# POOL's arithmetic moved to VectorE throughout a two-layer backbone, and a new order in the second half of the first layer's MLP

## The chip, the core and the metric

The kernel runs on one core of a Trainium2 chip. Its engines work side by side: TensorE (PE; its weight loads are listed apart as PEld), VectorE (DVE), ScalarE (ACT), GpSimd (POOL) and SyncE (SP). Each takes its own instructions strictly in order; waits between engines go over semaphores. A transfer is started by an instruction on one of the queues of SP, ACT or POOL and then runs by itself. The metric is the device time of one run in microseconds (us), as a median of several runs. Beside them there is one profiled execution, from which all durations of single instructions come.

## The reference

A backbone of two layers works on 1024 latent tokens (x) and 256 context tokens (ctx) of width 1024, all in fp32. Each layer computes, with adaLN shifts, scales and gates `m` from a conditioning vector (`mc` for the context, from a learned vector):

```python
h  = modulate(rmsnorm(x, g[0]), m[0], m[1]);  hc = modulate(rmsnorm(ctx, g[0]), mc[0], mc[1])
y, yc = mixer(h, hc, ...)       # layer 0: gated linear attention (GLA) | grouped-query attention with
                                # normed, rotated heads; layer 1: long convolution (hyena) | diff. attention
x = x + m[2] * rmsnorm(y, g[1])
x = x + m[5] * rmsnorm(sq_relu_mlp(modulate(rmsnorm(x, g[2]), m[3], m[4]), w_mlp_in[i], w_mlp_out[i]), g[3])
# layer 0 alone: the same two sums for ctx, with mc
def sq_relu_mlp(h, w1, w2): return jnp.square(jax.nn.relu(h @ w1)) @ w2    # 1024 -> 4096 -> 1024
```

Only x is returned.

## The kernel before

PE multiplies in a format (fp32r) that keeps fewer bits than fp32. So each fp32 operand is split in two: ACT rounds it to the high part, and another engine subtracts that from the source, which leaves the low part (`split`, L92 to L95). A product is then the sum of three matmuls, high by high, low by high, high by low (L103 to L105, L1515 to L1517). With a third argument `split` puts the subtraction on POOL, otherwise on DVE.

The stages follow one another along the span, with soft borders:

- 0 to 300 us: layer 0's norm, its input projection, the normed heads and their rotation. `head_norm` (L485 to L488) multiplies by the root mean square on DVE and by the gain on POOL; `rope` (L603 to L619) makes one product on DVE (L611), two half products on POOL (L616) and the sum of the two on POOL (L618). In these tiles `stg` is a block out of the projection, `rp_o` and `rp_u` are the rotated parts, `q_st` is the split result. In the same stage the adaLN weights (`w_ada`) are summed up on DVE, row block by row block (L259, L261; `ada_rest`), with the low part of the sum (`ada_hl`, L227) on POOL. This `ada` work goes on in the background of later stages.
- 300 to 600 us: grouped-query attention. 600 to 1000 us: the spectra of hyena's filters (`hy_m` blocks come by DMAs on POOL's queue), the GLA (`gl_ee`, L927, `gl_aT`, L960, `gl_sg`, L1004 and L1008, all on POOL) and the output projection.
- 1000 to 1464 us: the residual sum (`post_norm`, L1061, on POOL for every second tile), the norm, and the first half of layer 0's MLP (`up_...`), in a scheme of seven products over half blocks in place of eight. `s1` to `s4` are sums of weight blocks on DVE (L1223), whose space POOL's splits of the weights (`w_lo<-up_w`) must have left.
- 1476 to 1895 us: the second half, `mlp_down` (L1414). It takes the seven products in the order p1, p2, p3, p5, p6, p7, p4, each over 16 blocks k, which makes 112 steps. A step loads a block of the hidden values (`dn_h`), one or two blocks of weights (`dn_b`), for four of the products a block of the context's hidden values (`dn_c`), takes differences of weight blocks where the product needs one (L1477), splits both and multiplies for four tiles of 128 rows. `load(i)` runs `bufs[0]` steps ahead, `prep(i)` two steps ahead. The tuple `bufs` (5, 6, 4, 6) counts the buffers of raw hidden blocks, raw weight blocks, context blocks and split pairs. The first two steps' loads go on ACT's queue, the rest on SP's. At a product's last block `put` adds its four banks of PSUM into the sums in SBUF (`accx`, `accy`; L1496). PSUM has five banks with the tag `dp` for the x tiles and two with `cx` for the context, which takes part in p1, p2, p3 and p5 only. During p7 and p4 the generator `ends` runs once in two blocks: for the two context tiles (`accz`) and then the first four x tiles it does the norm, the gate (L1060) and the residual sum (L1061). `dn_t` is the weight block that p5 loads and p6 and p4 use again.
- 1895 to 2100 us: layer 1's projection, with `cb_lo` (the low part of a column block of weights, by `w_block`) and `qk_lo` on POOL. 2100 to 2400: differential attention; 2400 to 2700: the convolution (its `hm` blocks come by POOL's queue, the out-projection's weights are split into `wo_lo` on POOL); 2700 to 3058: out-projection and first half of the MLP; 3058 to 3385: its second half.

The order in which instructions stand on each engine isn't that of the code. It is worked out when the kernel is built, from the instructions' dependences and estimated durations, so an operation that goes to another engine moves others as well. A tile's space comes free when its last reader is done, and a transfer into it waits for that.

Of the kernel before, what the change touches and what calls it, by code (L numbers as in the profile page):

```python
# [91 lines left out]
def split(g, hi, lo, src, pool=False):  # L92

    g.nc.scalar.activation(hi, src, ACTF.Copy)  # L94
    (g.nc.gpsimd if pool else g.nc.vector).tensor_tensor(lo, src, f(hi), op=ALU.subtract)  # L95
# [369 lines left out]
def in_proj0(g, ps, ftp, vgp):  # L465
# [12 lines left out]
    with ExitStack() as st:  # L478
# [6 lines left out]
        def head_norm(src, nh, gain):  # L485
            r = head_rstd(g, pq[0], src, nh, 64, f"rp_u{nh}")
            nc.vector.tensor_tensor(src, src, r.unsqueeze(2).to_broadcast([128, nh, 64]), op=ALU.mult)
            nc.gpsimd.tensor_tensor(src, src, gain.unsqueeze(1).to_broadcast([128, nh, 64]), op=ALU.mult)  # L488
# [117 lines left out]
def rope(g, pool, src, nh, t1, t2):  # L606
# [8 lines left out]
    for k in range(2):  # L615
        nc.gpsimd.tensor_tensor(uv[:, :, :, k], sv[:, :, :, 1 - k],  # L616
                                tv[:, :, k].unsqueeze(1).to_broadcast([128, nh, 32]), op=ALU.mult)
    nc.gpsimd.tensor_tensor(o, o, u, op=ALU.add)  # L618
# [207 lines left out]
def gla(g, st, y_put):  # L826
# [81 lines left out]
    def weights(t, b, p, la):  # L908
# [18 lines left out]
        nc.gpsimd.tensor_tensor(gate(ee), gate(ee), kb, op=ALU.mult)  # L927
# [23 lines left out]
    def inner(t, b, ee, kinT):  # L951
# [8 lines left out]
        nc.gpsimd.tensor_tensor(aT, ab[b][:, :, 0, :], ab[b][:, :, 1, :], op=ALU.add)  # L960
# [89 lines left out]
def post_norm(g, y, x_t, gate, tmp, junk, pool=True):  # L1050
# [10 lines left out]
    (nc.gpsimd if pool else nc.vector).tensor_tensor(x_t, x_t, tmp, op=ALU.add)  # L1061
# [1529 lines left out]
```

## Time and profile before

| | |
|---|---|
| median of 3 runs | 3390.24 us (3385.76 to 3394.58) |
| profiled execution | 3387.06 us |
| its span in the trace | 3385.3 us |
| mean granted clock of PE | 0.967 |
| busy: ACT | 1538.6 us (45%) |
| busy: DVE | 2489.5 us (74%), 4507 instructions |
| transfers | 566.69 MB, 167 GB/s over the span |

A row of the profile names the line of the code, the engine, the operation, output and inputs by the program's names with their shapes, and how often it occurs; behind the bar stand the busy time, the mean duration of one in ns, and the idle time of the engine just before, with the engine or transfer that ended it. In a timeline a row begins with start and duration in us, and brackets hold the idle time before. "issue" in a chain of waits is time in which an engine waited for nothing that the profile shows.

### The profile page before, as it was taken

The page shows a single profiled execution, that of the slowest core. Times are in us where ns is not written, and L with a number is a line of the kernel's source. Part 1 is how long each engine was busy: PE and PEld are TensorE (multiplying, and loading weights), DVE is VectorE, ACT ScalarE, POOL GpSimd, SP SyncE. Part 2 cuts the span into 40 slices and gives each one's busy share as a digit, 9 for nine tenths or more (in the row PEclk, how much of TensorE's full clock was granted, in tenths as well). Part 3 has the DMA queues.
Part 4 walks back from the last instruction along what each step waited for, and adds up shares of the span by engine and source line. Part 5 has one row for each costly group of instructions (what it writes and reads, how often), then busy time and mean ns, then how long its engine had stood idle before and what let it go on. Part 6 is the DMA issues. An engine that isn't in the chain of part 4 may idle for free.

```text
span 3385.3 us, 41884 instructions
## 1 busy us (share of the span) xinstructions
PE 3134.7 (93%) x13896; PEld 2405.3 (71%) x13896; DVE 2489.5 (74%) x4507; ACT 1538.6 (45%) x3150; POOL 528.0 (16%) x392
## 2 busy tenths in 40 slices
PE   8879999889987999989998899999968989999998
PEld 4766777667766788868876777766635667887886
DVE  6787767677658776766688666677778489877777
ACT  4444766554655222223345543576621352224453
POOL 0153000123222122201111112100020122210000
PEclk9999999999998999999999999999989999999999
DMA  6544111667753343378777455432344635438964
GB/s 227 154 129 147 55 40 47 178 193 228 244 199 114 132 146 131 134 255 297 240 245 241 135 167 168 116 97 74 122 142 135 226 113 168 146 137 303 314 194 161
DMA packets 344581, 566.69 MB, mean 167 GB/s; under 512 B 43329, under 2 KB 138561, under 8 KB 344236
## 3 DMA queue, kind: packets, MB, share of 16 engines
q1 hardware_dynamic: 296244, 491.19, 44.4%
q10 hardware_dynamic: 40952, 47.67, 4.1%
q0 software_dynamic: 7168, 25.17, 2.5%
q8 instruction: 109, 1.79, 0.2%
q14 instruction: 108, 0.88, 0.1%
HBM read 410.36 MB, written 153.55 MB: 167 GB/s over the span
## 4 chain that ended last, share of the span: by engine, by line
PE 63%; DVE 14%; issue 10%; DMA 7%; ACT 3%; POOL 3%; SPq 0%; ACTq 0%; POOLq 0%; DVEq 0%
PE up_ps L105 5%; PE up_ps L104 5%; PE up_ps L103 5%; PE dn_ps L1516 5%; PE dn_ps L1515 5%; PE dn_ps L1517 5%; PE s_ps L644 2%; PE up_ps L1234 1%; PE s_ps L738 1%; PE o_ps L2224 1%; DMA up_w<-in_w_mlp_in 1%; PE st_ps L758 1%; PE st_ps L759 1%; DVE ada_acc L261 1%; PE o_ps L771 1%
## 5 line engine op out<-in xcount | busy, mean ns | idle before, releaser
L1515 PE MATMUL dn_ps<-dn_w_hi,dn_h_hi 128*128 128x512 f32 x896 | 351.3, 394 | 28.2 <-DVE accy L1496 14.3
L1516 PE MATMUL dn_ps<-dn_w_lo,dn_h_hi 128*128 128x512 f32 x896 | 352.9, 394 | 5.3 <-DVE dn_w_lo L95 5.3
L1517 PE MATMUL dn_ps<-dn_w_hi,dn_h_lo 128*128 128x512 f32 x896 | 351.5, 392 | 0.0
L94 ACT ACTIVATE dn_h_hi<-dn_h 128x512 fp32r<-128x512 f32 x224 | 140.8, 629 | 279.4 <-PE dn_ps L1516 192.1
L95 POOL TENSOR_TENSOR w_lo<-up_w,w_hi 128x512 fp32r<-128x512 f32 x106 | 144.4, 1372 | 582.8 <-ACT w_hi L94 548.1
L95 DVE TENSOR_TENSOR dn_h_lo<-dn_h,dn_h_hi 128x512 fp32r<-128x512 f32 x224 | 161.9, 723 | 83.7 <-ACT dn_h_hi L94 83.3
L1515 PEld LDWEIGHTS dn_ps<-dn_w_hi,dn_h_hi 128*128 128x128 f32 x896 | 169.8, 190 | 67.7 <-DVE accy L1496 16.1
L1516 PEld LDWEIGHTS dn_ps<-dn_w_lo,dn_h_hi 128*128 128x128 f32 x896 | 170.1, 190 | 43.6 <-DVE dn_w_lo L95 8.5
L1517 PEld LDWEIGHTS dn_ps<-dn_w_hi,dn_h_lo 128*128 128x128 f32 x896 | 170.1, 190 | 35.4
L261 DVE SCALAR_TENSOR_TENSOR ada_acc<-w_ada,sc,ada_acc 128x512 f32<-128x512 f32 x224 | 169.0, 791 | 19.7 <-DMA w_ada<-in_w_ada 19.0
L94 ACT ACTIVATE s_hi<-up_w 128x512 fp32r<-128x512 f32 x128 | 79.1, 630 | 192.6 <-DVE up_w L1223 113.3
L95 DVE TENSOR_TENSOR gq_lo<-gq_p,gq_hi 128x512 fp32r<-128x512 f32 x168 | 115.4, 690 | 55.9 <-ACT gq_hi L94 54.3
L105 PE MATMUL up_ps<-t_hi,s_lo 128*128 128x512 f32 x384 | 152.3, 398 | 2.4 <-DVE s_lo L95 2.4
L104 PE MATMUL up_ps<-t_lo,s_hi 128*128 128x512 f32 x384 | 152.0, 396 | 2.8 <-DVE t_lo L95 2.8
L103 PE MATMUL up_ps<-t_hi,s_hi 128*128 128x512 f32 x384 | 152.6, 397 | 1.4 <-ACT t_hi L94 1.3
L1223 DVE TENSOR_TENSOR up_w<-up_w 128x512 f32<-128x512 f32 x128 | 94.0, 737 | 79.0 <-POOL w_lo L95 77.2
L654 DVE TENSOR_REDUCE sm_m<-s_ps 128x1 f32<-128x512 f32 (+1 forms) x192 | 110.2, 595 | 44.7 <-PE s_ps L644 43.3
L95 POOL TENSOR_TENSOR ada_hl<-ada_acc,ada_hl 128x512 fp32r<-128x512 f32 x32 | 62.3, 1958 | 510.7 <-ACT ada_hl L94 359.4
L739 DVE TENSOR_REDUCE gq_mx<-s_ps 128x1 f32<-128x256 f32 (+1 forms) x208 | 112.2, 580 | 29.1 <-PE s_ps L738 28.2
L668 ACT ACTIVATE df_p<-s_ps,sm_m 128x512 f32<-128x512 f32 (+1 forms) x192 | 116.7, 618 | 34.5 <-DVE sm_m L658 31.1
L94 ACT ACTIVATE w_hi<-up_w 128x512 fp32r<-128x512 f32 x106 | 64.7, 628 | 142.4 <-DMA up_w<-in_w_mlp_in 63.5
L761 ACT ACTIVATE gq_p<-st_ps 128x512 f32<-128x512 f32 x168 | 99.7, 597 | 61.2 <-PE st_ps L759 60.3
(499 smaller groups left out, 8906.6 us busy)
## 6 DMA issues: line engine op xcount, KB each, us to landing
dn_b<-in_w_mlp_out SPq DMA_DIRECT2D x252, 256.0 KB
w_ada<-in_w_ada SPq DMA_DIRECT2D x96, 512.0 KB
up_w<-in_w_mlp_in SPq DMA_DIRECT2D x32, 1024.0 KB
hy_m<-in_k_ff POOLq DMA_DIRECT2D x32, 512.0 KB, 5.1
dn_c<-hidc SPq DMA_DIRECT2D x64, 256.0 KB
x<-x_in SPq DMA_DIRECT2D x26, 512.0 KB
x_in<-x SPq DMA_DIRECT2D x26, 512.0 KB
cb_raw<-in_od_w_in SPq DMA_DIRECT2D x20, 512.0 KB
```

Source lines behind the costliest of these rows:

```text
L94: g.nc.scalar.activation(hi, src, ACTF.Copy)
L95: (g.nc.gpsimd if pool else g.nc.vector).tensor_tensor(lo, src, f(hi), op=ALU.subtract)
L103: nc.tensor.matmul(out, ah, bh, start=(i == 0), stop=False)
L104: nc.tensor.matmul(out, ah, bl, start=False, stop=False)
L105: nc.tensor.matmul(out, al, bh, start=False, stop=(i == n - 1))
L261: nc.vector.scalar_tensor_tensor(acc[:, s], w[:, k], sc, acc[:, s], op0=ALU.mult, op1=ALU.add)
L654: nc.vector.tensor_reduce(m[:, i:i + 1], s, axis=AX.X, op=ALU.max)
L668: g.nc.scalar.activation(d, s, ACTF.Exp, bias=m, scale=0.125, accum_out=l[:, i:i + 1])
L739: nc.vector.tensor_reduce(mx[u][:, i, j:j + 1], ps, axis=AX.X, op=ALU.max)
L1515: nc.tensor.matmul(ps, hh[:, sl], wh, start=(k == 0), stop=False)
L1516: nc.tensor.matmul(ps, hh[:, sl], wl, start=False, stop=False)
L1517: nc.tensor.matmul(ps, hl[:, sl], wh, start=False, stop=(k == nb - 1))
```

## The change

It has two parts. First, each operation that POOL computes goes to DVE: the low parts that `split` put on POOL, those of the adaLN sums, the head gains, three of the four steps of the rotation, the four operations of the GLA, the residual sums. POOL keeps its memsets and DMA issues. Secondly, in `mlp_down` for layer 0:

- `bufs` goes from (5, 6, 4, 6) to (8, 9, 4, 4): more raw blocks, fewer split pairs.
- The `dn_t` tiles are allocated ahead, and the first two steps load on POOL's queue in place of ACT's.
- Two of p7's four tiles and one of p4's take a `cx` bank.
- The context's gate is loaded when p6 begins, and the context's two tiles are normed and added during p6 (`ctx_ends`); `ends` holds the x tiles alone.

```diff
-    (g.nc.gpsimd if pool else g.nc.vector).tensor_tensor(lo, src, f(hi), op=ALU.subtract)
+    g.nc.vector.tensor_tensor(lo, src, f(hi), op=ALU.subtract)
...
-            nc.gpsimd.tensor_tensor(src, src, gain.unsqueeze(1).to_broadcast([128, nh, 64]), op=ALU.mult)
+            nc.vector.tensor_tensor(src, src, gain.unsqueeze(1).to_broadcast([128, nh, 64]), op=ALU.mult)
...
-        nc.gpsimd.tensor_tensor(uv[:, :, :, k], sv[:, :, :, 1 - k],
+        nc.vector.tensor_tensor(uv[:, :, :, k], sv[:, :, :, 1 - k],
                                 tv[:, :, k].unsqueeze(1).to_broadcast([128, nh, 32]), op=ALU.mult)
-    nc.gpsimd.tensor_tensor(o, o, u, op=ALU.add)
+    nc.vector.tensor_tensor(o, o, u, op=ALU.add)
...
-        nc.gpsimd.tensor_tensor(gate(ee), gate(ee), kb, op=ALU.mult)
+        nc.vector.tensor_tensor(gate(ee), gate(ee), kb, op=ALU.mult)
...
-        nc.gpsimd.tensor_tensor(aT, ab[b][:, :, 0, :], ab[b][:, :, 1, :], op=ALU.add)
+        nc.vector.tensor_tensor(aT, ab[b][:, :, 0, :], ab[b][:, :, 1, :], op=ALU.add)
...
-    (nc.gpsimd if pool else nc.vector).tensor_tensor(x_t, x_t, tmp, op=ALU.add)
+    nc.vector.tensor_tensor(x_t, x_t, tmp, op=ALU.add)
...
+    if ctx:
+        ts = {k: rp.tile([128, 512], F32, name=f"dn_t{k}") for k in range(nb)}
...
-        q = nc.scalar if i < 2 else nc.sync
+        q = (nc.gpsimd if ctx else nc.scalar) if i < 2 else nc.sync
...
-        return [psa(g, [128, 512], name="dn_ps", tag="dp") for _ in range(n)]
+        tags = {"p7": ("dp", "cx", "cx", "dp"), "p4": ("dp", "dp", "dp", "cx")} if ctx else {}
+        return [psa(g, [128, 512], name="dn_ps", tag=tag) for tag in tags.get(n, ("dp",) * 4)]
...
-    ends = [done(t, zs[t]) for t in range(len(zs))] + [done(NC_T + t, xs[t]) for t in range(4)]
-    ends = pipelined(item(e) for e in ends)
+    ctx_ends = pipelined(item(done(t, zs[t])) for t in range(len(zs)))
+    ends = pipelined(item(done(NC_T + t, xs[t])) for t in range(4))
...
+            if n == "p6" and ctx:
+                gates.update({1: mod(g, p, layer, 5, (1,), name="gate")[0]})
...
+        if n == "p6" and k % 2:
+            next(ctx_ends, None)
...
-                                (norm, hs.__setitem__), 4, (5, 6, 4, 6))
+                                (norm, hs.__setitem__), 4, (8, 9, 4, 4))
```

The same replacement is made at `ada_hl`, `gl_sg` and in `w_block`. Three places in the new order follow. POOL's queue first, from the first half of layer 0's MLP to the projection of layer 1, as it was:

```order
L95 TENSOR_TENSOR w_lo<-up_w,w_hi 128x512 x57
L95 TENSOR_TENSOR ada_hl<-ada_acc,ada_hl 128x512 x14
L1061 TENSOR_TENSOR x_in<-x_in,accz_13914 128x1024
L1061 TENSOR_TENSOR x_in<-x_in,accx_13906 128x1024
L1061 TENSOR_TENSOR x_in<-x_in,accx_13908 128x1024
L1061 TENSOR_TENSOR x_in<-x_in,accy_13910 128x1024
L95 TENSOR_TENSOR w_lo<-w_raw,w_hi 128x1024
L1061 TENSOR_TENSOR x_in<-x_in,accy_13912 128x1024
L95 TENSOR_TENSOR w_lo<-w_raw,w_hi 128x1024
```

and as it is now, from the filters of layer 0 to the convolution of layer 1:

```order
L1884 DMA hy_m<-in_k_ff 128x1024 x32
L1454 DMA dn_h<-hid_0p_9557 128x512
L1464 DMA dn_b<-in_w_mlp_out 128x512
L1454 DMA dn_h<-hid_1p_9564 128x512
L1464 DMA dn_b<-in_w_mlp_out 128x512
L1990 DMA hm<-in_k_df 128x512 x8
L1990 DMA hm<-in_k_di 128x512 x4
```

No arithmetic is left in it. The two pairs of loads of `mlp_down` (`dn_h`, `dn_b`) stand right behind the 32 blocks `hy_m` and ahead of the first `hm`.

On DVE, the end of the context in `mlp_down`: `accz_13914` and `accz_13915` are the two context tiles, `dn_t_...` the weight blocks of p6. Before:

```order
L1060 SCALAR_TENSOR_TENSOR accz_13914<-accz_13914,rs_t,gate 128x1024
L1060 SCALAR_TENSOR_TENSOR accz_13915<-accz_13915,rs_t,gate 128x1024
L95 TENSOR_TENSOR dn_h_lo<-dn_h,dn_h_hi 128x512
L95 TENSOR_TENSOR dn_w_lo<-dn_t_16186,dn_w_hi 128x512
L1061 TENSOR_TENSOR x_in<-x_in,accz_13915 128x1024
L95 TENSOR_TENSOR dn_h_lo<-dn_h,dn_h_hi 128x512
```

and now:

```order
L1060 SCALAR_TENSOR_TENSOR accz_13914<-accz_13914,rs_t,gate 128x1024
L95 TENSOR_TENSOR dn_h_lo<-dn_h,dn_h_hi 128x512
L1061 TENSOR_TENSOR x_in<-x_in,accz_13914 128x1024
L95 TENSOR_TENSOR dn_w_lo<-dn_t_13928,dn_w_hi 128x512
L95 TENSOR_TENSOR dn_h_lo<-dn_h,dn_h_hi 128x512
L95 TENSOR_TENSOR dn_w_lo<-dn_t_13929,dn_w_hi 128x512
```

Before, the first context tile's sum was POOL's (above) and DVE came to the gates at the splits of p6's last such block, `dn_t_16186`. Now the gate and the sum stand between splits in the middle of p6, and the second tile's follow one block later.

On DVE, one tile of the rotation in layer 0's projection. Before:

```order
L487 TENSOR_TENSOR stg<-stg,rs_t 128x512
L628 TENSOR_REDUCE hr_ss<-hr_sq 128x8
L611 TENSOR_TENSOR rp_o<-stg,tq_329 128x512
L113 TENSOR_SCALAR rs_t<-hr_ss 128x8
L261 SCALAR_TENSOR_TENSOR ada_acc<-w_ada,sc,ada_acc 128x512
L116 SCALAR_TENSOR_TENSOR rs_t<-rs_t 128x8
L261 SCALAR_TENSOR_TENSOR ada_acc<-w_ada,sc,ada_acc 128x512
L117 TENSOR_TENSOR rs_t<-rs_t 128x8
L95 TENSOR_TENSOR q_st<-rp_o,q_st 128x8x64
L118 SCALAR_TENSOR_TENSOR rs_t<-rs_t 128x8
L261 SCALAR_TENSOR_TENSOR ada_acc<-w_ada,sc,ada_acc 128x512
L487 TENSOR_TENSOR stg<-stg,rs_t 128x512
```

and now:

```order
L611 TENSOR_TENSOR rp_o<-stg,tq_329 128x512
L116 SCALAR_TENSOR_TENSOR rs_t<-rs_t 128x8
L616 TENSOR_TENSOR rp_u<-stg,tq_330 128x256
L117 TENSOR_TENSOR rs_t<-rs_t 128x8
L616 TENSOR_TENSOR rp_u<-stg,tq_330 128x256
L118 SCALAR_TENSOR_TENSOR rs_t<-rs_t 128x8
L261 SCALAR_TENSOR_TENSOR ada_acc<-w_ada,sc,ada_acc 128x512
L487 TENSOR_TENSOR stg<-stg,rs_t 128x512
L618 TENSOR_TENSOR rp_o<-rp_o,rp_u 128x512
L95 TENSOR_TENSOR w_lo<-w_raw,w_hi 128x1024
L488 TENSOR_TENSOR stg<-stg,gq_gq 128x512
L95 TENSOR_TENSOR q_st<-rp_o,q_st 128x8x64
```

The two half products (L616), the sum (L618) and the gain (L488) now stand on DVE between the steps of the norm (L113 to L118), the weights' low parts and the sums of the adaLN weights (L261).

More of the change, by code (lines that the diff above doesn't have):

```diff
@@ L89, in psb, with split @@
     return psa(g, [128, 1024], name=name, tag="pb")
-def split(g, hi, lo, src, pool=False):
+def split(g, hi, lo, src, *_):
     g.nc.scalar.activation(hi, src, ACTF.Copy)
-    (g.nc.gpsimd if pool else g.nc.vector).tensor_tensor(lo, src, f(hi), op=ALU.subtract)
+    g.nc.vector.tensor_tensor(lo, src, f(hi), op=ALU.subtract)
 def mm3(g, out, terms):
@@ L226, in half @@
                 nc.scalar.activation(hi, src, ACTF.Copy)
-                nc.gpsimd.tensor_tensor(lo, src, f(hi), op=ALU.subtract)
+                nc.vector.tensor_tensor(lo, src, f(hi), op=ALU.subtract)
                 for w, x in enumerate((hi, lo)):
@@ L1003, in forward @@
         sgf = sg.rearrange("p h e -> p (h e)")
-        nc.gpsimd.tensor_scalar(sgf, gt, -80.0, None, op0=ALU.max)
+        nc.vector.tensor_scalar(sgf, gt, -80.0, None, op0=ALU.max)
         nc.scalar.activation(sgf, sgf, ACTF.Exp, scale=-1.0)
@@ L1007, in forward @@
         nc.scalar.activation(sgf, sgf, ACTF.Exp, scale=-1.0)
-        nc.gpsimd.tensor_tensor(sgf, sgf, gt, op=ALU.mult)
+        nc.vector.tensor_tensor(sgf, sgf, gt, op=ALU.mult)
         v = wk.tile([128, 4, 128], F32, name="gl_v", tag="gl_v")
@@ L1439, in mlp_down @@
     rp, p = (st.enter_context(g.tc.tile_pool(name=f"{n}{layer}", bufs=1, reuse_waits="tile")) for n in ("dr", "dn"))
-    raws, parts, cs, gates = {}, {}, {}, []
+    raws, parts, gates = {}, {}, {}
+    if ctx:
+        ts = {k: rp.tile([128, 512], F32, name=f"dn_t{k}") for k in range(nb)}
     where = dict(p1=(0, 0), p2=(1, 0), p3=(1, 1), p5=(0, 1)) if ctx else {}
@@ L1455, in load @@
             if n == "p5" and b == "b12":
-                w = ts[k] = p.tile([128, 512], F32, name=f"dn_t{k}")
+                if not ctx:
+                    ts[k] = p.tile([128, 512], F32, name=f"dn_t{k}")
+                w = ts[k]
             else:
@@ L1565, in mlp_down @@
         if k == 0:
-            ps = tiles(4)
+            ps = tiles(n)
             if n in ("p1", "p3") and ctx:
                 cps = [psa(g, [128, 512], name="dc_ps", tag="cx") for _ in range(2)]
+            if n == "p6" and ctx:
+                gates.update({1: mod(g, p, layer, 5, (1,), name="gate")[0]})
             if n == "p7":
                 run(bg)
-                gates.extend(mod(g, pool, layer, 5, range(2 - layer), name="gate", tag="gate", bufs=2))
+                gates.update({0: mod(g, pool, layer, 5, (0,), name="gate", tag="gate", bufs=2)[0]})
         for t in range(4):
@@ L1644, in w_block @@
             nc.scalar.activation(h[:, :, sl], v, ACTF.Copy)
-            (nc.vector if 2 > x else nc.gpsimd).tensor_tensor(l[:, :, sl], v, f(h[:, :, sl]), op=ALU.subtract)
+            nc.vector.tensor_tensor(l[:, :, sl], v, f(h[:, :, sl]), op=ALU.subtract)
     else:
```

## The prediction

> **What bounds the kernel now.** I read the page's busy times and chain first, then the stages one by one, since an average over 3385 us hides which stage waits for what. The page's first and fourth parts:
>
> ```profile
> PE 3134.7 (93%) x13896; PEld 2405.3 (71%) x13896; DVE 2489.5 (74%) x4507; ACT 1538.6 (45%) x3150; POOL 528.0 (16%) x392
> ...
> PE 63%; DVE 14%; issue 10%; DMA 7%; ACT 3%; POOL 3%; SPq 0%; ACTq 0%; POOLq 0%; DVEq 0%
> ...
> L95 POOL TENSOR_TENSOR w_lo<-up_w,w_hi 128x512 fp32r<-128x512 f32 x106 | 144.4, 1372 | 582.8 <-ACT w_hi L94 548.1
> ```
>
> TensorE (PE) is busy for 3134.7 us of 3385.3, so at most 250.6 us can be won without removing matmuls, and the change removes none. POOL works 528.0 us in 392 instructions and holds 3% of the chain. One low part of 128x512 costs POOL 1372 ns. The table of stretches (us from the span's start, then the busy time of PE, of weight loads, of DVE, ACT and POOL, each with its instructions, then the granted clock) tells where PE idles:
>
> ```profile
> 100.00:300.00 200.00, 166.24 (x843) 135.08 (x841) 161.36 (x328) 77.52 (x192) 90.39 (x80) 0.91 0.54 168
> 300.00:600.00 300.00, 298.34 (x1398) 225.42 (x1397) 218.62 (x427) 209.44 (x361) 0.95 (x1) 1.00 0.14 46
> 600.00:1000.00 400.00, 358.98 (x1720) 272.15 (x1719) 274.17 (x579) 220.32 (x494) 98.40 (x88) 0.96 0.68 214
> 1000.00:1100.00 100.00, 78.05 (x346) 62.26 (x346) 84.53 (x155) 58.80 (x120) 22.02 (x10) 0.90 0.34 117
> 1100.00:1464.00 364.00, 361.58 (x1663) 296.10 (x1661) 261.06 (x421) 92.58 (x179) 69.83 (x54) 1.00 0.38 135
> 1752.50:1796.20 43.70, 43.70 (x195) 35.89 (x193) 33.31 (x60) 20.34 (x42) 4.55 (x2) 1.00 0.66 209
> 1796.20:1805.00 8.80, 0.36 (x3) 0.01 (x1) 5.50 (x10) 4.84 (x9) 0.00 (x0) 0.76 0.85 283
> 1805.00:1851.50 46.50, 46.50 (x192) 37.95 (x192) 42.41 (x87) 29.03 (x61) 5.48 (x2) 0.94 0.78 255
> 1895.00:2100.00 205.00, 184.20 (x816) 146.10 (x814) 143.29 (x239) 94.22 (x186) 42.84 (x29) 0.95 0.48 147
> 2700.00:2900.00 200.00, 183.58 (x784) 143.92 (x784) 178.14 (x280) 78.69 (x142) 41.78 (x26) 0.97 0.42 143
> ```
>
> In 300 to 600 us (the attention of layer 0) and 1100 to 1464 us (the MLP's first half) PE is 99% busy, so nothing done beside it can gain much. In the projection before (100 to 300) PE lacks 33.8 us, in 600 to 1000 it lacks 41.0, in 1000 to 1100 22.0, in 1895 to 2100 20.8, in 2700 to 2900 16.4; and 1796.2 to 1805 is nearly empty: that is the seam between the products p6 and p7 of the second half of layer 0's MLP.
>
> **The price of an operation on either engine.** POOL's rope operations in 200 to 300 us, then quiet prices on DVE in 300 to 600 us (POOL does no work there, the table shows), then the same view in 1100 to 1400 us for an operand in PSUM, and in 200 to 300 us for a small operation:
>
> ```profile
> L616 POOL TENSOR_TENSOR rp_u<-stg,tq 128x256 f32<-128x256 f32 x16 | 19.6, 1245 | 4.7 <-DVE hr_ss L628 4.6
> L488 POOL TENSOR_TENSOR stg<-stg,gq_gq 128x512 f32<-128x512 f32 x8 | 17.8, 2228 | 14.4 <-DVE stg L487 9.6 <-ACT qT L549 4.9
> L618 POOL TENSOR_TENSOR rp_o<-rp_o,rp_u 128x512 f32<-128x512 f32 x8 | 12.7, 1585 | 2.0 <-DVE rp_o L611 1.5
> ```
> ```profile
> L95 DVE TENSOR_TENSOR gq_lo<-gq_p,gq_hi 128x512 fp32r<-128x512 f32 x147 | 100.9, 689 | 52.6 <-ACT gq_hi L94 51.4
> ...
> L791 DVE TENSOR_TENSOR gq_y<-gq_y,gq_rl 128x256 f32<-128x256 f32 x16 | 6.7, 420 | 0.3
> ...
> L744 DVE TENSOR_SCALAR gq_mr<-gq_m 128x4 fp32r<-128x4 f32 x18 | 3.0, 167 | 0.4
> ```
> ```profile
> L1343 DVE TENSOR_TENSOR up_u<-up_u,up_ps 128x512 f32<-128x512 f32 x48 | 32.7, 681 | 0.4
> ```
> ```profile
> L113 DVE TENSOR_SCALAR rs_t<-hr_ss 128x8 f32<-128x8 f32 x7 | 4.9, 703 | 0.1
> ```
>
> A low part takes DVE 689 ns against POOL's 1372: half. If all of POOL's 528.0 us were arithmetic, DVE would get at most 528.0 × 689/1372 = 265 us more. But POOL also costs DVE time. L113 is one scalar operation on 128x8 numbers; beside a POOL that is busy 45% of 100 to 300 us its mean is 703 ns, and an operation as small, L744, takes 167 ns in the quiet stage. The timelines of POOL and DVE at 1787 us show one such case:
>
> ```profile
> 1787.48 3.30 POOL L1061 TENSOR_TENSOR x_in<-x_in,accz 128x1024 f32<-128x1024 f32 x1 [33.73 <-DVE accz L1060]
> ```
> ```profile
> 1788.44 2.88 DVE L95 TENSOR_TENSOR dn_h_lo<-dn_h,dn_h_hi 128x512 fp32r<-128x512 f32 x1
> 1791.25 0.68 DVE L95 TENSOR_TENSOR dn_w_lo<-dn_t,dn_w_hi 128x512 fp32r<-128x512 f32 x1
> ```
>
> The low part at 1788.44 starts inside POOL's addition and ends half a microsecond after it, 2.88 us long; the next one takes 0.68. So 2.20 us of DVE went into 3.30 us of POOL. The Trainium skill, page "SBUF — State Buffer", section "🔬 SBUF: two separate sides", says that an operation of DVE with two SBUF inputs and a GpSimd operation that reads SBUF exclude each other for a whole instruction rather than share bandwidth. By that rule the trace agrees: 2.88 beside 3.30 us, while L1343, with one operand in PSUM, keeps 681 ns beside a POOL that is 19% busy. Under plain sharing of bandwidth no small operation would wait, the relief below would be near nothing, and the sum would be that of rival 4.
>
> From rows: relief is 2.20/3.30 = 0.67 us per us of POOL while DVE has work, and it has for 74% of the span: 0.67 × 0.74 × 528.0 = 261 us against 265 added. **Over the whole, DVE's busy time should stay about where it is**, 2490 us; as bounds for its net change I take −126 (every POOL microsecond blocks DVE while it has work: 0.74 × 528.0 = 391 of relief) to +265 (no relief). What the change can win is then latency: a step on the path takes half as long and crosses no second engine.
>
> **X, POOL's arithmetic to DVE, stage by stage.** The chains of waits in 100 to 300, 690 to 760 and 1895 to 2100 us, and two rows of the waits of the whole run:
>
> ```profile
> by line: DVE ada_acc L261 15.3%; issue 13.5%; DMA gk<-kT 6.3%; POOL rp_u L616 5.7%; POOL rp_o L618 5.1%; DMA w_ada<-in_w_ada 4.9%; DMA w_raw<-in_ev_w_in 4.9%; POOL stg L488 4.6%; DVE q_st L95 2.7%; DVE w_lo L95 2.2%; DVE stg L487 1.9%; PE v
> ```
> ```profile
> by line: issue 74.5%; POOL gl_aT L960 10.2%; POOL gl_ee L927 7.4%; POOL hy_m L1875 6.4%; PE sp_ps L105 1.3%; PE sp_ps L104 1.3%; PE sp_ps L103 1.0%; POOLq L1875 0.2%; POOLq L927 0.1%; POOLq L960 0.1%
> ```
> ```profile
> by line: issue 13.6%; PE pj_ps L104 6.9%; PE pj_ps L103 6.8%; PE pj_ps L105 6.7%; DMA w_ada<-in_w_ada 6.4%; POOL qk_lo L95 4.8%; DVE qk_u L1747 4.1%; PE qk_ps L1655 3.0%; PE qk_ps L1657 2.9%; PE qk_ps L1656 2.7%; DMA cb_raw<-in_od_w_in 2.6%
> ```
> ```profile
> DVE up_w L1223 <- POOL w_lo L95: 77.2, 24, 9.4
> ```
>
> - Projection and rope, 100 to 300: POOL's three lines are 5.7 + 5.1 + 4.6 = 15.4% of 200 us, 31 us of the chain. A tile costs POOL 2.228 + 2 × 1.245 + 1.585 = 6.30 us; on DVE, at 689 ns for the two of 128x512 and 420 (L791's size) for the halves, 2 × 0.689 + 2 × 0.420 = 2.22 us. That would take 65% of 31 = −20. But the steps now queue on DVE behind the sums of L261 (15.3% of the same chain). I take half, **−10**; ends −20 and +6 (each of 8 tiles waits for one more 0.7 us operation).
> - 600 to 1100: gl_aT and gl_ee are 17.6% of 70 us = 12.3 us of the chain; half goes: **−6**. Ends 0 (DVE, 69% busy there, is not free at that moment) and −20 (half of the 41.0 us in which PE lacks work).
> - 1895 to 2100: qk_lo is 4.8% of 205 us = 9.8; half would be −5. DVE works on the same columns, so I take **−3**, ends +6 and −10.
> - 1100 to 1464, and the like in layer 1: DVE waits 77.2 us for POOL's w_lo, but PE is 99% busy there. The cover is the lead of DVE's splits over PE, and DVE's share of 72% leaves room: **0**.
> - 2700 to 2900 is the tight one: DVE 178.14 of 200. Added 41.78/2 = 20.9, relief 0.67 × 0.89 × 41.78 = 24.9. Ends −4 and +21; near the relief, with something for weight splits that stand ahead of evictions: **+3**.
>
> X: −10 − 6 − 3 + 0 + 3 = **−16**.
>
> **Y, the second half of layer 0's MLP.** Three seams. The timeline around the first (p1 begins), with ACTq the DMA issues of ACT's queue, and in brackets what ended the idle time:
>
> ```profile
> 1466.36 0.42 ACT L94 ACTIVATE up_c<-up_r 128x256 fp32r<-128x256 f32 x1 [1.80 <-DVE up_r L1239]
> ...
> 1468.42 0.51 ACTq L1460 DMA_DIRECT2D dn_b<-in_w_mlp_out  x1
> ...
> 1474.77 0.63 ACT L94 ACTIVATE dn_h_hi<-dn_h 128x512 fp32r<-128x512 f32 x1 [7.99 <-DMA dn_b<-in_w_mlp_out]
> ...
> 1476.60 0.80 PE L1515 MATMUL dn_ps<-dn_w_hi,dn_h_hi 128*128 128x512 f32 x1 [12.44 <-ACT dn_w_hi L94]
> ```
>
> PE is idle for 12.44 us. The first weights are issued at 1468.42, because their space came free with the last stores, and land 6 us later. With preallocated tiles and the loads on POOL's queue, which now has only transfers ahead of it, they wait only until weight sums of the last of the 16 blocks have left their space; a block takes 364/16 = 23 us, so as an estimate they are issued 10 us or more before the first half ends. Next late is ACT: it ends the context's split at 1466.78, then splits hidden and weight block (0.63 each), so PE starts near 1468.1: **−8**. Ends 0 (POOL's two pairs come late; the third step's on SP's queue still stand behind the last stores) and −12.4. Moving the pair off ACT's queue also spares ACT four issues, which shortens nothing. At the other two seams, DVE and PE rows:
>
> ```profile
> 1786.05 2.48 DVE L1060 SCALAR_TENSOR_TENSOR accz<-accz,rs_t,gate 128x1024 f32<-128x1024 f32 x2 [3.23 <-DMA gate<-mods]
> ...
> 1803.05 0.69 DVE L1477 TENSOR_TENSOR dn_b<-dn_b 128x512 f32<-128x512 f32 x1 [2.83 <-DMA dn_b<-in_w_mlp_out]
> ```
> ```profile
> 1804.99 0.79 PE L1515 MATMUL dn_ps<-dn_w_hi,dn_h_hi 128*128 128x512 f32 x1 [8.44 <-DVE accy L1496]
> ```
> ```profile
> 1855.15 0.65 PE L1515 MATMUL dn_ps<-dn_w_hi,dn_h_hi 128*128 128x512 f32 x1 [3.56 <-DVE accy L1496]
> ```
>
> Here the context's norm waits for its gate (3.23 us), a weight difference waits for its block (2.83), both on DVE, and behind them stand the evictions that p7's first matmul waits for: 8.44 us. After the idle time PE is slow: 46.50 us for 192 matmuls against 43.70 for 195 in p6, at a clock of 0.94 against 1.00: 3.5 us more. With two of p7's tiles in banks that the context left, and 8 and 9 raw blocks on the way instead of 5 and 6, three tiles start without an eviction: −9 of 8.44 + 3.5 = 11.9. Into p6 comes the context's sum that POOL did (1.4 us, as two operations of 128x512): DVE has 33.31 us in 43.70 there, room for it and for what follows it. p7 has 42.41 in 46.50, and gains two residual sums that POOL did (2 × 1.4): nearly full, so not all is won. **−9**, ends 0 and −11.9. From p7 to p4, 3.56 us with one tile more in a free bank: **−2**, ends 0 and −3.6. Y: −8 − 9 − 2 = **−19**.
>
> **The sum.** −16 − 19 = −35 on the profiled 3387.06 us: 3352. The median of the runs is 3390.24, 3.2 above the profiled one, so the forecast is 3390 − 35 = **3355**.
>
> **Rivals.**
> 1. *DVE is no faster for the queue* (X nets 0: what a step saves it waits for on DVE). For it: L261 in the chain of 100 to 300. Against it: the 703 ns row. 3390 − 19 = 3371.
> 2. *The idle time goes at its outer ends*: Y −28, rope −20, GLA −12, qk −5: −65, 3325. For it: chains that cross POOL lose two hand-overs; against it: "issue" holds 74.5% of the GLA chain.
> 3. *X costs what Y gives*: DVE 89% busy in 2700 to 2900 pays +21 and X loses elsewhere nothing: 3390 − 19 + 21 = 3392, no change.
> 4. *Slower: DVE becomes the bound because the relief does not come.* Then each stretch that is tight grows until DVE's share is again the 0.89 of 2700 to 2900: there (178.1 + 20.9)/0.89 − 200 = +23; 100 to 300: (161.4 + 45.2)/0.89 − 200 = +32; 1000 to 1100: (84.5 + 11.0)/0.89 − 100 = +7. +62 − 19 = +43: 3433. It decides on L113: if its 703 ns stay, this holds; at about 170 it falls. The Trainium skill, page "Perfetto Trace Analysis", section "Optimizing Scalar/DVE Operations", speaks for this rival: a saturated DVE may hand work to GpSimd, and this change does the reverse. By that rule a DVE at 74% would lose; the same passage warns that the two share a read port, so the hand-over may not help, which the row of 2.88 us bears out.
>
> That the change would not do what it says is excluded by POOL's new order, in which only memsets and DMA issues stand.
>
> **Numbers.** Chances: forecast 0.42 (its own range 3340 to 3368), rival 1 0.21, rival 2 0.15, rival 3 0.12, rival 4 0.10. A measurement here tells 0.3% (10 us) from no change. Faster: 0.42 + 0.21 + 0.15 = 0.78; same 0.12; slower 0.10. The range leaves out rival 4 and a tenth at the outer end of rival 2 and beyond rival 3: 3318 to 3394.
>
> **What would show it.** Right: L113 on 128x8 near 170 ns; DVE's busy time 2400 to 2560; the seams near 4, 3 and 2 us; PE's busy time unchanged or a little lower with the clock. Wrong: DVE over 2650 us, PE waiting for DVE in 2700 to 2900 or 100 to 300 for longer than now, or a first matmul of p1 that waits for a load on POOL's queue.

## The result, and the profile after

The kernel takes 3332.3 us (median of 4 runs, 3329.68 to 3336.66) against 3390.12 before: a ratio of 0.9828, 95% interval 0.9814 to 0.9843. That is 58 us less, where 35 were forecast. The profiled execution has a span of 3330.2 us at the same mean clock, 0.967. The page, first and fourth part:

```profile
PE 3125.3 (94%) x13896; PEld 2403.8 (72%) x13896; DVE 2519.0 (76%) x4825; ACT 1546.6 (46%) x3150; POOL 42.0 (1%) x78
...
PE 76%; DVE 12%; DMA 5%; ACT 3%; issue 3%; SPq 0%; ACTq 0%; POOL 0%; DVEq 0%; POOLq 0%
```

Of the 55 us by which the span is shorter, PE's busy time gives 9 and its idle time 46. DVE went from 2489.5 to 2519.0 us, POOL from 528.0 to 42.0. PE now holds 76% of the chain instead of 63%, POOL nothing, "issue" 3% instead of 10%. DVE's rows in the projection of layer 0 (190 to 285 us, the rotation's operations now among them):

```profile
L261 DVE SCALAR_TENSOR_TENSOR ada_acc<-w_ada,sc,ada_acc 128x512 f32<-128x512 f32 x40 | 28.3, 742 | 1.2 <-DMA w_ada<-in_w_ada 1.2
L616 DVE TENSOR_TENSOR rp_u<-stg,tq 128x256 f32<-128x256 f32 x16 | 6.2, 417 | 0.0
L488 DVE TENSOR_TENSOR stg<-stg,gq_gq 128x512 f32<-128x512 f32 x9 | 6.1, 682 | 0.0
...
L618 DVE TENSOR_TENSOR rp_o<-rp_o,rp_u 128x512 f32<-128x512 f32 x8 | 5.4, 678 | 0.0
...
L113 DVE TENSOR_SCALAR rs_t<-hr_ss 128x8 f32<-128x8 f32 x8 | 1.3, 164 | 0.0
```

L113 on 128x8 takes 164 ns instead of 703, L261 742 instead of 822. A tile's rotation costs 0.682 + 2 × 0.417 + 0.678 = 2.19 us on DVE, as priced (2.22), where POOL took 6.30.

Where the time went is read from the same instruction in each trace: the start of the first (or last, where it says so) matmul of a stage. The table gives it before in us, and how much earlier (−) it comes after and in four of the experiments below.

Each column is one profiled execution, and small steps in it can be chance. Up to 1450 us the instructions of after and x_only, and of the later kernels lo_first, no_spare_banks, ctx_in_p7 and old_buffers, stand in the same order on PE and DVE; yet their traces lead by 17.4 to 23.1 us at the attention, and lose 3.0 to 9.2 from the filters to the transposes. A step under some 5 us says little. The profiled execution of y_only was the slowest of its eight, 3 us above their median, so its last rows show too little gain.

| start of | before | after | x_only | y_only | rope_only | lows_dve |
|---|---|---|---|---|---|---|
| layer 0's attention (L738) | 298.3 | −18.8 | −19.2 | −0.9 | −15.9 | −7.2 |
| hyena's filters (L1862) | 622.1 | −15.9 | −15.0 | −0.5 | −13.3 | −5.9 |
| transposes ahead of the out-projection (L1144) | 944.2 | −10.3 | −12.0 | −0.4 | −10.4 | −5.6 |
| MLP up, products t with w (L103) | 1085.5 | −17.4 | −20.6 | +0.9 | −11.7 | −15.9 |
| MLP up, its last (L1234) | 1463.6 | −18.1 | −21.3 | +1.5 | −10.8 | −18.9 |
| p1, first by the low part (L1516) | 1477.3 | −20.9 | −20.2 | −1.8 | −11.5 | −19.6 |
| p5, the context's last (L1526) | 1751.0 | −20.9 | −19.3 | +6.2 | −11.3 | −16.4 |
| layer 1's first transpose (L383) | 1899.7 | −37.1 | −29.4 | −4.6 | −11.2 | −21.2 |
| its projection, the context's last (L103) | 1953.8 | −42.6 | −36.6 | −5.7 | −11.3 | −23.4 |
| hyena's columns (L1655) | 2099.8 | −50.5 | −41.9 | −7.4 | −12.5 | −30.9 |
| the out-projection's last (L103) | 2716.5 | −52.2 | −42.4 | −8.3 | −11.1 | −29.3 |
| MLP up, products t with w, last (L103) | 3054.1 | −51.9 | −42.7 | −5.3 | −11.2 | −28.7 |
| end of the span | 3385.3 | −55.1 | −45.5 | −2.0 | −9.2 | −27.2 |

Four places carry it: 19 us ahead of the attention, 7 ahead of the MLP (after 5.6 had been lost from the filters to the transposes), 22 from p5's end to layer 1's projection, 8 in layer 1's columns. The seam before p1 gave 3. From p5's end to the columns these are the rows (p6, p7 and p4; the start of layer 1's projection; its columns), before and then after:

```profile
1751.50:1899.70 148.20, 136.20 (x580) 111.25 (x579) 116.74 (x216) 75.58 (x152) 13.42 (x5) 0.95 0.67 222
1899.70:1979.00 79.30, 69.57 (x322) 56.28 (x321) 48.16 (x101) 50.61 (x107) 7.07 (x3) 0.94 0.31 96
1979.00:2099.80 120.80, 109.73 (x474) 85.78 (x473) 90.97 (x134) 41.69 (x75) 33.18 (x25) 0.96 0.61 187
```

```profile
1730.60:1862.70 132.10, 131.63 (x581) 108.39 (x580) 113.75 (x220) 81.00 (x159) 0.00 (x0) 1.00 0.66 222
1862.70:1936.40 73.70, 66.84 (x322) 55.12 (x321) 44.33 (x103) 46.94 (x104) 0.00 (x0) 0.95 0.33 103
1936.40:2049.20 112.80, 107.24 (x473) 84.28 (x472) 96.72 (x155) 41.02 (x74) 0.00 (x0) 0.98 0.66 198
```

From p6 to p4 PE is 99.6% busy at a clock of 1.00; the idle 8.44 and 3.56 us are gone but for 0.47 us at p4's start. As many matmuls take 131.63 us instead of 136.20 at 0.95, which is half of what PE's busy time lost. DVE is 86% busy there, and PE hardly waits for it. The seam before p1, PE's row and DVE's:

```profile
1449.76 0.96 PE L1519 MATMUL dn_ps<-dn_w_hi,dn_h_hi 128*128 128x512 f32 x2 [3.71 <-ACT dn_w_hi L94]
1456.41 0.79 PE L1520 MATMUL dn_ps<-dn_w_lo,dn_h_hi 128*128 128x512 f32 x1 [5.70 <-DVE dn_w_lo L95]
```
```profile
1449.21 0.69 DVE L95 TENSOR_TENSOR dn_h_lo<-dn_h,dn_h_hi 128x512 fp32r<-128x512 f32 x1
1455.27 0.49 DVE L259 TENSOR_SCALAR ada_acc<-w_ada,sc 128x512 f32<-128x512 f32 x1 [5.37 <-DMA w_ada<-in_w_ada]
1455.68 0.68 DVE L95 TENSOR_TENSOR dn_w_lo<-dn_b,dn_w_hi 128x512 fp32r<-128x512 f32 x1
```

The first matmul comes after 3.71 us of idle time, as forecast (4). But DVE's next row is the first sum of adaLN weights, which waits 5.37 us for its transfer, and the low part that the second group of matmuls needs stands behind it: PE idles for another 5.70.

### The profile page after: what moved, and what is told of

It reads as the page before. It is cut to its first block, busy times and chain, and to the rows that moved or that the text cites. A ratio compares the mean times of both kernels' runs of the same rounds, so it can differ in the third digit from the quotient of the medians.

```text
span 3330.2 us, 41432 instructions
## 1 busy us (share of the span) xinstructions
PE 3125.3 (94%) x13896; PEld 2403.8 (72%) x13896; DVE 2519.0 (76%) x4825; ACT 1546.6 (46%) x3150; POOL 42.0 (1%) x78
## 4 chain that ended last, share of the span: by engine, by line
PE 76%; DVE 12%; DMA 5%; ACT 3%; issue 3%; SPq 0%; ACTq 0%; POOL 0%; DVEq 0%; POOLq 0%
PE up_ps L105 6%; PE up_ps L103 6%; PE up_ps L104 6%; PE dn_ps L1520 6%; PE dn_ps L1521 6%; PE dn_ps L1519 6%; PE s_ps L644 2%; PE o_ps L2233 2%; PE up_ps L1234 2%; PE fa_ps L2004 1%; PE y_ps L2004 1%; DVE ada_acc L261 1%; PE pj_ps L103 1%; PE pj_ps L104 1%; PE pj_ps L105 1%
## 5 line engine op out<-in xcount | busy, mean ns | idle before, releaser
L95 DVE TENSOR_TENSOR dn_h_lo<-dn_h,dn_h_hi 128x512 fp32r<-128x512 f32 x224 | 154.0, 687 | 78.2 <-ACT dn_h_hi L94 77.4
L1520 PEld LDWEIGHTS dn_ps<-dn_w_lo,dn_h_hi 128*128 128x128 f32 x896 | 169.4, 189 | 51.3 <-DVE dn_w_lo L95 16.4
L261 DVE SCALAR_TENSOR_TENSOR ada_acc<-w_ada,sc,ada_acc 128x512 f32<-128x512 f32 x224 | 160.0, 746 | 20.5 <-DMA w_ada<-in_w_ada 19.9
L103 PE MATMUL up_ps<-t_hi,s_hi 128*128 128x512 f32 x384 | 152.1, 396 | 1.6 <-ACT s_hi L94 1.6
L668 ACT ACTIVATE df_p<-s_ps,sm_m 128x512 f32<-128x512 f32 (+1 forms) x192 | 116.8, 619 | 29.3 <-DVE sm_m L658 25.8
L95 DVE TENSOR_TENSOR dn_w_lo<-dn_b,dn_w_hi 128x512 fp32r<-128x512 f32 x160 | 109.7, 686 | 11.6 <-ACT dn_w_hi L94 11.3
L94 ACT ACTIVATE dn_w_hi<-dn_b 128x512 fp32r<-128x512 f32 x160 | 99.5, 622 | 39.1 <-PE dc_ps L1532 27.6
L95 DVE TENSOR_TENSOR s_lo<-up_w,s_hi 128x512 fp32r<-128x512 f32 x128 | 87.6, 686 | 27.6 <-ACT s_hi L94 27.6
```

Source lines behind the costliest of these rows:

```text
L95: g.nc.vector.tensor_tensor(lo, src, f(hi), op=ALU.subtract)
L103: nc.tensor.matmul(out, ah, bh, start=(i == 0), stop=False)
L261: nc.vector.scalar_tensor_tensor(acc[:, s], w[:, k], sc, acc[:, s], op0=ALU.mult, op1=ALU.add)
L668: g.nc.scalar.activation(d, s, ACTF.Exp, bias=m, scale=0.125, accum_out=l[:, i:i + 1])
L1520: nc.tensor.matmul(ps, hh[:, sl], wl, start=False, stop=False)
```

## The experiments

The theory with which they were made: the two parts add up, each where the trace of after gains. Ratios are to the kernel before, measured beside it, with 95% intervals; the microseconds won or lost are worked out from them.

**The two parts alone.** x_only has POOL's arithmetic on DVE and the second half of the MLP as before; y_only the reverse.

```diff
 x_only: the lines of the change outside mlp_down and its call, such as
-    nc.gpsimd.tensor_tensor(o, o, u, op=ALU.add)
+    nc.vector.tensor_tensor(o, o, u, op=ALU.add)
 y_only: the lines in mlp_down and its call, such as
-                                (norm, hs.__setitem__), 4, (5, 6, 4, 6))
+                                (norm, hs.__setitem__), 4, (8, 9, 4, 4))
```

> POOL's arithmetic on DVE alone; the second half of the MLP as before. Theory (the two parts add up, each where the trace of after gains): about 17 us up to the MLP's second half, 8 in layer 1's projection, 4 behind it, so 3390 - 29 = 3361. Rival (the order's part works only because DVE is free of POOL, or the other way round): x_only under 10 us, above 3380, or nearly the whole gain, under 3345.

> The new second half of the MLP alone; arithmetic of POOL stays. Theory (parts add up): the seam before p1 gains 2 to 3 us, those at p6, p7, p4 and behind it some 15 to 22: 3390 - 22 = 3368. Rival (POOL's residual sums block DVE in p6 and p7, so that the new order alone brings little): above 3380.

Measured: x_only 3340.17 us, 0.9847 (0.9831 to 0.9863), 52 us less; y_only 3382.34, 0.9971 (0.9961 to 0.9982), 10 less. The sum of 62 is near the 58 of both, but it isn't split as the theory had it: the arithmetic brings five times what the new order brings, and at the seams the two gains overlap. In x_only, whose second half of the MLP is the old one, this is the PE row with idle time ahead where p7 begins:

```profile
1779.10 0.50 PE L1515 MATMUL dn_ps<-dn_w_hi,dn_h_hi 128*128 128x512 f32 x1 [0.53 <-DVE accy L1496]
```

The seam that idled for 8.44 us idles for 0.53, with the old banks, the old buffers and the context still in p7. The new order alone clears it as well: in y_only PE waits for no more than 0.45 us around p7's start and for 1.17 at p4's. By the table, from p5's end to layer 1's first transpose x_only wins 10.1 us, y_only 10.8 and both together 16.2, so a part of what either brings there the other brings too. y_only then wins 1.1 more up to the projection's last matmul, x_only 7.2. And y_only loses 8.0 us between p1 and p5, where x_only loses 0.8 and after nothing. Part of that are direct waits for POOL's low parts of the adaLN sums, 2.2 us in these two rows; what the rest is stays open:

```profile
1511.13 0.63 PE L277 MATMUL ada_ps<-ada_hl,colsr 128*2 128x512 f32 x2 [1.16 <-POOL ada_hl L95]
1512.80 0.40 PE L277 MATMUL ada_ps<-ada_hl,colsr 128*2 128x512 f32 x1 [1.04 <-POOL ada_hl L95]
```

**Which of POOL's operations.** Each of four kernels is the one before with one kind on DVE.

```diff
 rope_only: L488, L616, L618    ada_dve: L227    sums_dve: L1061    lows_dve: L92, L95, L1645, such as
-    (g.nc.gpsimd if pool else g.nc.vector).tensor_tensor(lo, src, f(hi), op=ALU.subtract)
+    g.nc.vector.tensor_tensor(lo, src, f(hi), op=ALU.subtract)
```

> Of the first part only the heads' gain and the rotation (three operations per tile) go to DVE. Theory (the hand-overs to POOL in these chains were the loss of the first stage): attention begins 15 us earlier, 3375. Rival (the weights' and adaLN sums' low parts were what held the stage): under 5 us, above 3385.

> Before, with the low parts of the adaLN sums alone on DVE. Theory (on POOL one of them took 9.99 us just ahead of p6, so the context's gate came late and DVE's queue stood before it at the seam to p7): the gate comes earlier, the seam's idle 8.4 us shrink to 2 or 3, 3390 - 7 = 3383. Rival (at that seam DVE stands at the load of a weight block anyway): 2 us or nothing, 3388.

> Before, with the residual sums alone on DVE. Theory (each sum on POOL took 2.4 to 3.3 us, held DVE as long, and stood in the chain from p4 to layer 1's projection and to the norm ahead of the MLP): 3390 - 7 = 3383, most of it between p7 and the first transposes of layer 1 and some before the MLP. Rival (others of POOL's operations did that): 2 us or nothing.

> Before, with the low parts that split and w_block gave to POOL on DVE: weights of the MLP's first halves, x_lo, ftc, cb_lo, qk_lo, uh_lo, wo_lo. Theory (x_lo and qk_lo stood in chains; the weights' low parts gain nothing, being hidden): 6 us before the MLP, 6 in layer 1's projection, 3390 - 12 = 3378. Rival (140 more operations on a DVE that still shares with POOL's other work cost what they bring): 3390 or more.

Measured: rope_only 3376.3 us, 0.9956 (0.9944 to 0.9968); ada_dve 3391.72, 1.0004 (0.9994 to 1.0013); sums_dve 3370.83, 0.9939 (0.9925 to 0.9952); lows_dve 3359.76, 0.9909 (0.9894 to 0.9924). So −15, +1 (which its interval doesn't tell from 0), −21 and −31 us. The edit at L1645 moves nothing, since its condition chose DVE before too. The rotation came out as expected, with attention 15.9 us earlier. That the adaLN low parts held the gate was wrong, and the time is that of the rival. The sums brought three times the expectation and the low parts two and a half times. PE's rows at the seam to p7, in the order ada_dve, sums_dve, lows_dve:

```profile
1805.68 0.80 PE L1515 MATMUL dn_ps<-dn_w_hi,dn_h_hi 128*128 128x512 f32 x1 [7.18 <-DVE accy L1496]
```
```profile
1801.05 0.80 PE L1515 MATMUL dn_ps<-dn_w_hi,dn_h_hi 128*128 128x512 f32 x1 [4.75 <-DVE accy L1496]
```
```profile
1784.04 0.79 PE L1515 MATMUL dn_ps<-dn_w_hi,dn_h_hi 128*128 128x512 f32 x1 [3.92 <-DVE accy L1496]
```

8.44 us became 7.18, 4.75 and 3.92. Two things in the traces go with this. One is POOL's sum of the first context tile, which took 3.30 us before and held a low part of DVE for 2.88, with the eviction that PE waited for behind it; in sums_dve and x_only it is on DVE, while lows_dve keeps it (2.72 us, beside a low part of 2.88). The other is the context's gate. DVE's rows that wait for it, in sums_dve, lows_dve and x_only:

```profile
1785.04 2.48 DVE L1060 SCALAR_TENSOR_TENSOR accz<-accz,rs_t,gate 128x1024 f32<-128x1024 f32 x2 [1.79 <-DMA gate<-mods]
```
```profile
1763.08 1.28 DVE L1060 SCALAR_TENSOR_TENSOR accz<-accz,rs_t,gate 128x1024 f32<-128x1024 f32 x1 [2.30 <-DMA gate<-mods]
```
```profile
1759.82 1.29 DVE L1060 SCALAR_TENSOR_TENSOR accz<-accz,rs_t,gate 128x1024 f32<-128x1024 f32 x1 [1.66 <-DMA gate<-mods]
```

DVE goes on with the gate 10.5 us ahead of p6's end before, 11.4 in ada_dve and 11.3 in sums_dve, but 17.0 in lows_dve and 18.8 in x_only. Neither the sum on DVE (sums_dve) nor the earlier gate (lows_dve) clears the seam alone; x_only has both, and 0.53 us is left. In ada_dve the gate hardly moves, so this run doesn't test what the gate does to the seam. No run moves the gate alone, and why it comes earlier in lows_dve and x_only stays open. A late DVE also makes itself later: by the trace of before, the load for which DVE waits 2.83 us at this seam waited itself for DVE's difference at 1797.12 us, and was started at 1797.84, when that was done. The four kinds sum to −66, more than x_only's −52; whether they overlap or the GLA's four operations cost on DVE what is missing wasn't tried alone.

**Is it the port?** Two kernels add operations on POOL, whose results nobody uses, to layer 0's attention of the kernel after, where POOL is idle. The two tiles `extra` are filled once ahead, which the cut leaves out; the order on PE, DVE and ACT is that of after throughout.

```diff
 pool_reads:
+            if kt % 2:
+                nc.gpsimd.tensor_tensor(extra[1], extra[0], extra[0], op=ALU.add)
 pool_writes:
+            if kt % 2:
+                nc.gpsimd.memset(extra[1], 0.0)
```

> After, with 80 or so additions of 128x512 on POOL (one operand read twice from SBUF, the result used by nobody) in the attention of layer 0, where DVE's low parts take 690 ns alone. Theory (an operation of POOL that reads SBUF and one of DVE with two SBUF operands exclude each other): the mean of gq_lo rises by some 300 ns or more, that of gq_mx with its operand in PSUM stays at 680; about 0.67 us of DVE per us of POOL while DVE works. Rival (no exclusion; small prices beside POOL are waits for other reasons): gq_lo stays under 750 ns.

> As pool_reads, but POOL's operations fill 128x512 with zeros and read nothing. Theory (what excludes is reading SBUF on both sides): gq_lo stays at 690 ns beside them and gq_mr at 170. Rival (any operation of POOL holds DVE): gq_lo beside POOL near 1050 as in pool_reads.

POOL waits for nothing in these, so they stand in one run at the stage's start, 280 to 384 us in pool_reads and 274 to 323 in pool_writes. DVE's rows in 298 to 387 us beside the reading ones, where POOL is 91% busy, then in 280 to 320 us beside the filling ones, where it is 90% busy:

```profile
L95 DVE TENSOR_TENSOR gq_lo<-gq_p,gq_hi 128x512 fp32r<-128x512 f32 x40 | 41.9, 1053 | 8.4 <-ACT gq_hi L94 8.2
L739 DVE TENSOR_REDUCE gq_mx<-s_ps 128x1 f32<-128x512 f32 x30 | 19.4, 676 | 0.0
...
L797 DVE TENSOR_TENSOR gq_y<-gq_y,gq_rl 128x256 f32<-128x256 f32 x4 | 4.0, 1010 | 0.1
L744 DVE TENSOR_SCALAR gq_mr<-gq_m 128x4 fp32r<-128x4 f32 x5 | 3.8, 761 | 0.1
...
L796 DVE TENSOR_TENSOR gq_y<-ot_ps,gq_y 128x252 f32<-128x252 f32 x4 | 1.7, 414 | 0.9 <-ACT gq_y L795 0.9
...
L743 DVE TENSOR_REDUCE gq_m<-gq_mx 128x4 f32<-128x12 f32 x4 | 0.6, 152 | 0.0
```
```profile
298.00:387.00 89.00, 84.04 (x376) 60.04 (x375) 76.30 (x113) 57.45 (x99) 80.72 (x64) 1.00 0.14 47
```
```profile
L95 DVE TENSOR_TENSOR gq_lo<-gq_p,gq_hi 128x512 fp32r<-128x512 f32 x18 | 12.2, 686 | 2.3 <-ACT gq_hi L94 2.1
...
L744 DVE TENSOR_SCALAR gq_mr<-gq_m 128x4 fp32r<-128x4 f32 x3 | 1.0, 336 | 0.1
```
```profile
280.00:320.00 40.00, 39.56 (x182) 29.87 (x181) 32.00 (x62) 25.59 (x44) 36.04 (x70) 1.00 0.12 37
```

Beside reads, gq_lo takes 1053 ns instead of 689, gq_y from two SBUF tiles (L797, L791 before) 1010 instead of 420, and gq_mr on 128x4, with one SBUF tile and almost no data, 761 instead of 167. The operations with an operand in PSUM keep their price: gq_mx 676, the gq_y of L796 414. So does the reduction L743, whose one tile is in SBUF: 152 instead of 159. From 290 to 590 us gq_lo starts 43 times inside one of POOL's operations, with a mean of 1088 ns and up to 1527, and 101 times outside, never above 696. Beside fills gq_lo takes 686, as the theory has it, but gq_mr does not stay at 170: its three rows there take 379, 407 and 221 ns, against 161 to 172 in the 15 that follow between 330 and 590 us. A fill holds it too, for less time. Of the attention's lead, pool_reads loses 14 us (−19.5 to −5.6 us against before, from its start to the GLA's first transposes), though PE needs no result of POOL. Each of the two was run once (3344.38 and 3327.06 us). So the low parts came out as the theory has it. Two numbers of pool_reads were put wrongly. The mean of gq_lo from 290 to 590 us, forecast at +300 ns, is 808, since the operations covered a third of the stage. And 102.9 us of reading on POOL lengthened DVE's operations by 19.4 us in all, 0.19 us per us of POOL instead of some 0.67 with DVE 86% busy.

**The new order, piece by piece.** Three kernels undo one piece each in the kernel after.

```diff
 no_spare_banks:
-        tags = {"p7": ("dp", "cx", "cx", "dp"), "p4": ("dp", "dp", "dp", "cx")} if ctx else {}
+        tags = {}
 ctx_in_p7: the context's tiles back at the head of ends
-    ends = pipelined(item(done(NC_T + t, xs[t])) for t in range(4))
+    ends = pipelined(item(e) for e in [done(t, zs[t]) for t in range(len(zs))] + [done(NC_T + t, xs[t]) for t in range(4)])
 old_buffers:
-                                (norm, hs.__setitem__), 4, (8, 9, 4, 4))
+                                (norm, hs.__setitem__), 4, (5, 6, 4, 6))
```

> After, with all tiles of p7 and p4 in the five banks of before. Theory (the free banks let p7 start without an eviction): the idle 8.4 and 3.6 us at the two seams come back, 3332 + 11 = 3343. Rival (the eviction came late because DVE's queue stood at a gate and a load, and that has gone by the earlier context and the deeper buffers): 4 us at most, 3336.

> After, with the context's norms and sums during p7 as before, at the head of the tiles; its gate is still loaded at p6. Theory (free banks carry the seam): DVE gets 6 us more into p7, which was nearly full, 3332 + 4 = 3336. Rival (the context's place is what clears the seam): the seam idles 6 us or more, 3340 and above.

> After, with the buffer counts of before (5, 6, 4, 6). Theory (the deeper loads matter at the seam before p7 alone): 3332 + 3 = 3335. Rival 1 (they carry the gain): 3340 and above. Rival 2 (they do nothing): 3332.

Measured: no_spare_banks 3337.25 us, 0.9843 (0.9826 to 0.986); ctx_in_p7 3332.57, 0.983 (0.9809 to 0.9851); old_buffers 3330.92, 0.9826 (0.9809 to 0.9844). The deeper buffers and the place of the context make no difference that can be told once POOL is out of the way. The loads on POOL's queue weren't undone alone. The spare banks may be worth 5 us, about the rival's figure, with intervals that overlap; without them 0.73 us of idle time stand at p4's start, not the old 8.44 and 3.56.

**The second wait before p1.** lo_first makes the first adaLN sum depend on the low part that it stood ahead of.

```diff
+            if g.first_lo is not None:
+                nc.vector.tensor_copy(acc[:, :, 0], f(g.first_lo)[:, 0:2])
+                g.first_lo = None
```

> After, with one tiny copy that makes the first adaLN sum of the MLP's second half depend on the low part of the second step's weights, so that it can't stand ahead of it in DVE's order. Theory (in after DVE waits 5.37 us at this place for the adaLN weights, with the low part behind it): the 5.70 us of idle PE go, 3332 - 5 = 3327. Rival (the third step's loads are next late): 1 us or nothing.

Measured: 3328.65 us, 0.9816 (0.9803 to 0.983), beside 0.9828 (0.9814 to 0.9843) for after: faster by 4 us in the medians, which the intervals don't tell apart. PE's rows with idle time in 1440 to 1470 us are two:

```profile
1447.97 0.79 PE L1523 MATMUL dn_ps<-dn_w_hi,dn_h_hi 128*128 128x512 f32 x1 [3.72 <-ACT dn_w_hi L95]
1458.69 0.50 PE L1524 MATMUL dn_ps<-dn_w_lo,dn_h_hi 128*128 128x512 f32 x1 [0.27 <-DVE dn_w_lo L96]
```

The 5.70 us are gone there, and in the profiled execution, at the first matmul by the low part the kernel leads by 28.5 us instead of 20.9; ahead of layer 1's hyena columns by 53.3 instead of 50.5; and at the first output of its attention (2179.7 us before) by 42.0 instead of 42.1. So the mechanism held. In this execution, the slowest of its four at 3332.87 us, nearly all of it was given back behind it; whether the others gave it back isn't shown, since their median is 4 us lower.

## Why the prediction came out as it did

The direction held, the measured time lies in the outer range, and the signs came out: L113 at 164 ns, DVE at 2519 us, PE a little lower. But 3332 us is below the forecast's own range (3340 to 3368) and nearer to rival 2 (3325), whose terms aren't what happened either: it has −28 for Y, which brought 6 to 10, −12 for the GLA, where no gain shows, and −5 for qk_lo in a stretch that won 13. The size fell short, 35 for 58 us, and the split between the parts was the wrong way round: X was put at −16 and measured −52 alone, Y at −19 and measured −10 alone and some −6 on top of X (with intervals that overlap).

- *DVE's load.* "Over the whole, DVE's busy time should stay about where it is" held: +29.5 us. In part that is luck, since both terms were too large. The 318 operations that came from POOL take 220 us on DVE in the trace of after, added up one by one, where 265 was the most; and the durations of DVE's other 4507 add up to 2584 us instead of 2731, a relief of 147 us where 261 had been worked out from one row. (Operations in a row overlap a little, so the busy time rose by less than the 73 us that lie between these two.) That is 0.30 us per us of POOL instead of 0.67 × 0.74 = 0.50. Rival 4 fell by its own test (L113 at 164 ns). The passage of the Trainium skill that it names (page "Perfetto Trace Analysis", section "Optimizing Scalar/DVE Operations") speaks of a DVE that is saturated, so it doesn't say that one busy for 74% would lose. The Trainium skill, page "SBUF — State Buffer", section "🔬 SBUF: two separate sides", gives the rule that the relief rests on: operations of DVE with two SBUF inputs are held only by an operation of POOL that reads SBUF, those in a two-port mode by any. The runs agree in three points: 1053 beside reads, 686 beside fills, 676 for a PSUM operand. L744 with its one input is held beside both (761, and 221 to 407 beside fills), as the rule has it for a two-port mode; in which mode it runs the traces don't show.
- *Projection and rope, "I take half, −10".* The full share of the chain was right: −18.8, −15.9 of it by the rotation alone. The halving was for a queue on DVE behind L261. L261 itself fell from 822 to 742 ns (746 in rope_only), which fits a queue that got shorter.
- *600 to 1100, −6.* −1.5 in sum: 5.6 us lost up to the out-projection and 7 won ahead of the MLP. The traces with the same order lose 3.0 to 9.2 in the first part, and rope_only, whose GLA is on POOL, loses 3 there too, so nothing of the GLA's share of the chain shows as a gain. The win ahead of the MLP goes with the low parts (lows_dve −10.3) and less with the sums (sums_dve +1.8 to −2.9, 4.8).
- *First halves of the MLP, 0.* −0.8 in layer 0 and about 0 in layer 1: the waits of DVE for POOL's w_lo were hidden, as argued.
- *Seam before p1, −8.* −2.8. The start of p1 was as forecast; the step that failed was "next late is ACT": it was DVE's queue, with a sum that waits for a transfer. lo_first shows it.
- *Seams behind p6, −11, by the new order.* As a forecast of the new order alone this held: y_only wins 10.8 us from p5's end to layer 1's first transpose. What failed is the sum around it. X was put at nothing there and wins 10.1 without the new order (8.44 us become 0.53), so the two overlap at 16.2; and Y's 8.0 us lost between p1 and p5, beside a POOL that still works, were no term at all. The row for X's part stood in the prediction, as the price of POOL's 3.30 us to DVE's low part; it was used for DVE's total alone, and not at the one place where DVE's queue held PE.
- *1895 to 2100, −3.* This term is mis-sized most: −13.4 from layer 1's first transpose to its columns, past the outer end of −10. x_only alone gives −12.5 there and lows_dve −9.7. The forecast went by qk_lo alone, halved, where all of POOL's operations in the stretch went to DVE.
- *2700 to 2900, +3.* From the out-projection's last matmul to the last products: +0.3.

## What to carry to other kernels

An operation that is moved to a slow engine for relief has two prices: its own latency in the chain, and what it takes from the engine that it was to relieve. Here POOL spared VectorE 220 us and took 147 of them back, and its latency stood on PE's path at several seams. When an engine's small operations take four times their quiet price, look for what runs beside them; and where a wait goes, read what stands next in that engine's queue, transfers above all.
